# Projections of a hybrid trunk in four blocks of 448 columns and one of 288, in place of five of 416

## The chip, the cores and the metric

The kernel runs on one core of a Trainium2 chip. The metric is the device time of one launch in microseconds. A time is the median of several runs; beside it stands one profiled execution, whose trace is the source of all durations here.

## The reference

One layer of an encoder trunk, on T = 2080 rows of width 1024 (2048 prompt rows, 32 sample rows with their own history), all in fp32:

```python
hn = rmsnorm(h, g_mix)
proj = hn @ w_in                                   # 1024 x 3072
hA, bA, cA, zA, vB, zB = split(proj)               # six parts of 512
u = cA * hA                                        # conv mixer
yA = bA * (causal width-3 conv of u + bias) * silu(zA)
pooled = trailing mean of vB over 2/4/8/16 rows, by group of 128 channels, minus vB
yB = (pooled @ pool_w per group) * pool_scale * silu(zB)
h = h + concat[yA, yB] @ w_out
h = h + (p @ w_ple) * sigmoid(rmsnorm(h, g_ple) @ w_gate)
y = rmsnorm(h, g_final)
```

It also returns the last rows of u and v as states.

## The kernel before

**Numbers in two parts.** Every operand of a large matmul is split into a high and a low part (`split`, L77 to L79: ACT casts the high part, line 78; VectorE subtracts, line 79). A product of a 128-row slice is three matmuls (high by high, high by low, low by high). TensorE is named PE in the profile, with its weight loads as PEld.

**First stage, the projections.** The rows of x lie as columns in SBUF (normalised, transposed by `turn`, L416), in five blocks of `NB` = 416 columns. A block has three chunks of 128 rows and a short one of 32 (`x_rows`); the short chunks of two blocks share one tile (`columns_in`). A unit is one index j of four, that is 128 channels of each of the six parts zb, v, c, h, za, b. Blocks are taken in groups, `GROUPS = [[0, 1], [2, 3], [4]]`.

- Unit 0 of group 0 is computed as it stands (`plain`): 24 matmuls for each part and block (`project`, L581 and L564), 288 in all. Between its products the generator `second` prepares block 1, and `vectors` transposes the small vectors and splits the pool weights, all four groups of them at once (`pw`).
- The other seven units of groups 0 and 1 take both blocks of the pair at once by Strassen-Winograd (`seven`, `pair`): for each of the pairs (zb, v), (c, h), (za, b) seven half-products of 12 matmuls, 252 in a unit. Their right sides are six B pieces in three slots of the pool `acts`, and a seventh, T4, in `w7`. Names x_zbv, y_zbv, z_zbv and so on in the profile are these half-products' PSUM tiles.
- Group 2 is the last block alone, 384 prompt rows and the 32 sample rows, again by `plain`: 144 matmuls in a unit, in the order zb, v, c, h, the pool mixer's matmuls `pm` (method `mix`, L724 to L726), za, the states' transpose `pst`, b. Its columns were prepared by `last_block` beside group 1, chunk by chunk, and stored to memory (`b_d`); `hn_4` is read back at the start of group 2 by two loads on the POOL queue (L1140).

Within `plain` the pool mixer runs so: ACT copies v from PSUM to `V`; VectorE forms windowed sums (`win`, L746), `pl` (L758), and `pl` is split into `pp` (high and low part side by side in one tile); then `mix` multiplies by `pw` (three matmuls) and VectorE scales the result into `zs` (L728). The conv mixer multiplies h by c into `U` (L831), convolves (L771, L773), and multiplies by za and b (L844, L855). `store` writes `c_s` and `zs` to `y_d`.

VectorE and ACT also split each weight 10 us or so ahead of its use (`weights`, `put`; a ring of seven tiles), and in group 2 they form the sums of the output weights (`early_sums`, `weight_sums` L178) and the embedding weights `wp`.

**Later stages.** The output projection reads `y_d` back and does the same seven products with 512-wide matmuls (L168), then the embedding product (L103) and the gate follow. The change doesn't touch them, except that the first loads for the output stage (`load_y`, `load_rows`, `load_top`, pool `ya`) stand on the SP queue at the start of group 2.

The order of the instructions on each engine is set by a scheduler from the program; `keep_in_program_order` pins some of them. Every pool tile waits for the last readers of what lay there before; frames such as `frames_in` are closed to give their space to others.

## Time and profile before

| | |
|---|---|
| median of 3 runs | 922.03 us (920.8 to 922.24) |
| profiled execution | 923.96 us |
| its span, first to last instruction | 922.2 us |
| mean granted TensorE clock | 0.998 |
| 16.5 to 68.9 us | unit 0 |
| 68.9 to 426.4 us | the other seven units of groups 0 and 1 |
| 426.4 to 538 us | group 2, four units of about 27.9 us |
| 538 to 922 us | output projection, embedding, gate |

In a row of the windows stand, for each engine, the busy time and the number of instructions. In a row of the chain or the timeline stand the start, the length (from the first start to the last end of a run of like instructions) and their number; in brackets the idle time of the engine before them and what ended it. In the groups by line stand the busy time, the mean duration of one in ns, and the idle time before. A matmul's duration is longer than the distance between two starts, since matmuls are pipelined.

### The profile page before, as it was taken

Reading aid. Unit: us, or ns where it says so; the run is one execution under the profiler, and the core shown is the slowest. Engines: PE = TensorE matmul, PEld = TensorE weight load, DVE = VectorE, ACT = ScalarE, POOL = GpSimd, SP = SyncE. Lnnn points to the kernel's source line nnn. Section 1 sums busy time; section 2 is a strip of 40 time slices with the busy share of each in tenths; the row PEclk is TensorE's granted clock in tenths of the full one; section 3 lists DMA queues with packets and bytes.
Section 4 is the critical chain, followed back from the end, with each engine's and each line's share of the span. In section 5 each row is a group of like instructions: output and inputs, shape, how many; then the busy total and the mean of one; then the engine's idle time right before and its main releaser. Section 6 shows DMA issues by size and latency. Waiting matters only on the chain.

```text
span 922.2 us, 12940 instructions
## 1 busy us (share of the span) xinstructions
PE 907.6 (98%) x4485; PEld 820.7 (89%) x4485; DVE 723.1 (78%) x1231; ACT 477.8 (52%) x883; POOL 149.9 (16%) x271
## 2 busy tenths in 40 slices
PE   7999999999999999999999999999999999999996
PEld 5999999999999999999999987888877868888885
DVE  6896999999488989785777679665554799888975
ACT  6744565555335555443545456334334776465555
POOL 3111322212001111000000010111111002233333
PEclk9999999999999999999999999999999999999999
DMA  8345585769945546457655359755675876799883
GB/s 245 94 150 155 151 264 165 210 197 306 421 119 167 185 156 190 109 178 272 202 172 172 124 192 292 255 194 175 246 229 159 299 259 156 182 235 239 200 259 108
DMA packets 140734, 186.37 MB, mean 202 GB/s; under 512 B 12060, under 2 KB 111260, under 8 KB 139389
## 3 DMA queue, kind: packets, MB, share of 16 engines
q1 hardware_dynamic: 120237, 126.33, 44.7%
q0 software_dynamic: 17696, 53.71, 19.9%
q10 hardware_dynamic: 2736, 5.51, 1.8%
q8 instruction: 35, 0.57, 0.3%
q14 instruction: 30, 0.25, 0.1%
HBM read 128.93 MB, written 56.56 MB: 201 GB/s over the span
## 4 chain that ended last, share of the span: by engine, by line
PE 96%; ACT 1%; DVE 1%; DMA 1%; issue 0%; POOL 0%; SPq 0%; ACTq 0%; DVEq 0%; POOLq 0%
PE x_g L168 9%; PE x_o L168 9%; PE x_zbv L564 7%; PE x_ch L564 7%; PE x_zab L564 7%; PE e L103 5%; PE z_g L168 5%; PE z_o L168 4%; PE z_zbv L564 3%; PE z_ch L564 3%; PE z_zab L564 3%; PE v L564 3%; PE c L564 3%; PE b L564 3%; PE za L564 3%; PE h L564 3%
## 5 line engine op out<-in xcount | busy, mean ns | idle before, releaser
L78 ACT CAST y_S<-y_fS 128x512 fp32r<-128x512 f32 x32 | 19.5, 621 | 41.3 <-PE x_o L168 17.4
L103 PE MATMUL e<-wq,pps 128*128 128x512 f32 (+1 forms) x156 | 38.9, 399 | 0.2 <-ACT pps L78 0.2
L168 PE MATMUL x_o<-wo_b,y_S 128*128 128x512 f32 x128 | 35.7, 391 | 0.0
L168 PE MATMUL x_g<-wg_b,g_S 128*128 128x512 f32 x128 | 35.7, 389 | 0.0
L564 PE MATMUL z_zbv<-B,w_zbv_S 128*128 128x416 f32 x168 | 34.2, 352 | 0.0
L564 PE MATMUL x_ch<-B,w_ch_S 128*128 128x416 f32 x168 | 34.1, 351 | 0.0
L564 PE MATMUL z_zab<-B,w_zab_S 128*128 128x416 f32 x168 | 34.1, 351 | 0.0
L564 PE MATMUL x_zab<-B,w_zab_S 128*128 128x416 f32 x168 | 34.0, 351 | 0.0
L564 PE MATMUL x_zbv<-B,w_zbv_S 128*128 128x416 f32 x168 | 34.0, 351 | 0.0
L564 PE MATMUL z_ch<-B,w_ch_S 128*128 128x416 f32 x168 | 34.0, 350 | 0.0
L103 PEld LDWEIGHTS e<-wq,pps 128*128 128x128 f32 (+1 forms) x156 | 27.4, 182 | 6.9 <-ACT pps L78 0.5
L1396 POOL DMA_DIRECT2D e<-h_d x28 | 24.8, 907 | 51.1 <-DVE e L1393 42.3
L564 PEld LDWEIGHTS x_zab<-B,w_zab_S 128*128 128x128 f32 x168 | 31.3, 188 | 0.4
L564 PEld LDWEIGHTS x_zbv<-B,w_zbv_S 128*128 128x128 f32 x168 | 31.4, 188 | 0.3
L564 PEld LDWEIGHTS z_ch<-B,w_ch_S 128*128 128x128 f32 x168 | 31.4, 188 | 0.3
L564 PEld LDWEIGHTS z_zab<-B,w_zab_S 128*128 128x128 f32 x168 | 31.3, 188 | 0.3
L564 PEld LDWEIGHTS x_ch<-B,w_ch_S 128*128 128x128 f32 x168 | 31.3, 188 | 0.3
L564 PEld LDWEIGHTS z_zbv<-B,w_zbv_S 128*128 128x128 f32 x168 | 31.3, 188 | 0.4
L70 POOL TENSOR_SCALAR ms_x<-ssq_x 128x1 f32<-128x1 f32 (+2 forms) x18 | 10.7, 593 | 125.1 <-ACT junk L89 125.0
L78 ACT CAST y<-y 128x512 fp32r<-128x512 f32 x24 | 14.9, 619 | 29.3 <-PE z_o L168 12.8
L78 ACT CAST g_S<-g_fS 128x512 fp32r<-128x512 f32 x32 | 19.0, 618 | 18.6 <-DVE g_fS L1572 12.8
L168 PEld LDWEIGHTS x_o<-wo_b,y_S 128*128 128x128 f32 x128 | 24.0, 188 | 5.1 <-ACT c_o L1199 0.3
(592 smaller groups left out, 2656.6 us busy)
## 6 DMA issues: line engine op xcount, KB each, us to landing
y<-y_d SPq DMA_DIRECT2D x16, 512.0 KB, 5.6
x<-in_x_prompt_dram SPq DMA_DIRECT2D x16, 512.0 KB, 5.3
h_d<-x SPq DMA_DIRECT2D x16, 512.0 KB, 2.6
hn<-h_d SPq DMA_DIRECT2D x61, 128.0 KB, 6.5
xt<-in_x_prompt_dram SPq DMA_DIRECT2D x15, 512.0 KB, 6.1
e<-e_d SPq DMA_DIRECT2D x15, 512.0 KB, 6.0
e<-h_d POOLq DMA_DIRECT2D x28, 256.0 KB, 6.4
out_dram<-e POOLq DMA_DIRECT2D x13, 512.0 KB, 4.0
```

Source lines behind the costliest of these rows:

```text
L70: nc.gpsimd.tensor_scalar(ms[:n], ssq[:n], scalar1=1.0 / D, scalar2=EPS, op0=ALU.mult, op1=ALU.add)
L78: ins = nc.scalar.copy(hi, src)
L103: nc.tensor.matmul(ps[:n], pps[:, a, k, :n], wp[k][b][:, cs], start=k + q == 0, stop=k == 1 and q == 2)
L168: nc.tensor.matmul(ps[:n], lhs[:, k, a, :n], w[b][:, k], start=start and k + q == 0, stop=k == KH - 1 and q == 2, skip_group_check=True)
L564: nc.tensor.matmul(ps[:, :NB], lhs[:, k, x], b[:, k, y], start=start and k + q == 0, stop=stop and k == KH - 1 and q == 2, skip_group_chec ...
L1396: nc.gpsimd.dma_start(ee, h_d[r:r + P, at[1] * NH:at[1] * NH + NH], accum_op=ALU.add)
```

## The change

- `NB` is 448. The short chunk has `SH` = 64 rows; the last block has `NL` = 288 columns, two chunks of 128 prompt rows and the 32 sample rows, and `last_block` loops over three chunks, not four.
- The pool `acts` is closed with `frames_in` at the start of group 2 and opened again as `acts2` with smaller slots. T4 of the output weights has its eighth strip there (class `Strips`). The pools `acts2` and `ya` are opened with `reuse_waits="tile"`.
- The pool weight is loaded and split once for each unit (`load_pool_weight`, `pool_weight`). The low part of the pooled operand lies in a tile of the ring `e` (in group 2 behind the high part).
- In unit 0 `mix(0)` stands ahead of `v_block(1)`.
- `gm_row` lies in the ring `raws`; the staged short chunks take four tiles.

```diff
 EPS = 1e-6
-NB = 416
+NB = 448
+SH = NB - 3 * P
+NL = T - 4 * NB
 GROUPS = [[0, 1], [2, 3], [4]]
...
     w7 = ctx.enter_context(tc.tile_pool(name="w7", bufs=1))
-    SLOT = KC * 2 * NB
-    PIECE = SLOT // 2
+    PIECE = KH * 2 * NB
     def slot(name):
-        return acts[0].tile([P, SLOT], F32R, tag="hn", name=name)
+        return acts[-1].tile([P, 3 * KH * NH if len(acts) > 1 else 2 * PIECE], F32R, tag="hn", name=name)
+    class Strips:
+        def __init__(self, strips):
+            self.strips = strips
+        def __getitem__(self, at):
+            assert at[0] == slice(None)
+            return self.strips[at[1]]
...
     def seventh(name):
-        return w7.tile([P, 2 * KH * NH], F32R, tag="h", name=name)
+        return w7.tile([P, PIECE], F32R, tag="h", name=name)
...
         a, b = halves(slot(f"{name}_a")), halves(slot(f"{name}_b"))
-        t4 = seventh(f"{name}_T4").rearrange("p (h k n) -> p h k n", h=2, k=KH)
-        return dict(T1=a[:2], T2=(a[2], b[0]), T3=b[1:], T4=(t4[:, 0], t4[:, 1]))
+        t4 = seventh(f"{name}_T4")
+        t4 = [t4[:, i * NH:(i + 1) * NH] for i in range(2 * KH - 1)]
+        t4.append(acts[-1].tile([P, NH], F32R, tag="strip", bufs=1, name=f"{name}_T4_strip"))
+        return dict(T1=a[:2], T2=(a[2], b[0]), T3=b[1:], T4=(Strips(t4[:KH]), Strips(t4[KH:])))
...
         raws = pool("raws", 4)
-        acts.append(ctx.enter_context(tc.tile_pool(name="acts", bufs=3, side="right")))
         frames_in = ExitStack()
+        acts.append(frames_in.enter_context(tc.tile_pool(name="acts", bufs=3, side="right")))
         xin = frames_in.enter_context(tc.tile_pool(name="xin", bufs=5, side="right"))
...
-        gm_row = wk.tile([P, 2, 2 * NB], F32, tag="pp", bufs=1, name="gm_row").rearrange("p h n -> p (h n)")[:1, :D]
+        gm_row = ring4(raws, "gm_row")[:1]
         nc.sync.dma_start(gm_row, g_mix)
...
             r = tb * NB + c * P
-            if c < 3:
-                return x_p[r:r + P]
-            return x_p[r:r + DEC] if tb < 4 else x_s
+            if tb == 4:
+                return x_p[r:r + P] if c < 2 else x_s
+            return x_p[r:r + (P if c < 3 else SH)]
...
                     t = turn(xs[0], half, f"pt_{tag}_{half}", later=True)
-                    yield [t[:, :, :DEC], t[:, :, DEC:2 * DEC]]
+                    yield [t[:, :, :SH], t[:, :, SH:2 * SH]]
...
                 yield
-            n = P if len(xs) == 2 else DEC
+            n = P if len(xs) == 2 else SH
             f12, f1, f21 = (ftile(f"{c}_{tag}")[:, :, :n] for c in ("f12", "f1", "f21"))
...
         p_d = {q: tc.dram_tile([P, KH, 2, NB], F32, name=f"p_d{q}") for q in NAMES}
-        b_d = tc.dram_tile([P, KC, 2, NB], F32, name="b_d")
+        b_d = tc.dram_tile([P, KC, 2, NL], F32, name="b_d")
...
                 for q, (x, y) in enumerate(((0, 0), (0, 1), (1, 0))):
-                    nc.tensor.matmul(ps[:, :NB], lhs[:, k, x], b[:, k, y], start=start and k + q == 0,
+                    nc.tensor.matmul(ps[:, :b.shape[-1]], lhs[:, k, x], b[:, k, y], start=start and k + q == 0,
                                      stop=stop and k == KH - 1 and q == 2, skip_group_check=True)
...
             normal(x)
-            n = P if c < 3 else DEC
+            n = P if c < 3 else SH
             for half, q in enumerate(("11", "21")):
...
                 normal(x, True)
-            xs.append((short0, slice(DEC, 2 * DEC)))
+            xs.append((short0, slice(SH, 2 * SH)))
             yield
...
         vec = const.tile([P, 112], F32, name="vec")
-        pw = one.tile([P, 2, 4, P], F32R, name="pw")
+        pw_raws = []
+        def load_pool_weight(j):
+            t = one.tile([P, P], F32, tag="pw_raw", name=f"pw_raw_{j}")
+            nc.sync.dma_start(t, pool_w[0, j])
+            pw_raws.append(t)
+        def pool_weight(j):
+            t = one.tile([P, 2, P], F32R, tag="pw", name=f"pw_{j}")
+            split(t[:, 0], t[:, 1], pw_raws.pop())
+            load_pool_weight((j + 1) % 4)
+            return t
         rows = ftile("rows").rearrange("p k n -> p (k n)")[:112, :P]
...
             nc.vector.tensor_copy(vec, pv[:, :112])
-            split(pw[:, 0], pw[:, 1], pw_raw)
...
-        pw_raw = raws.tile([P, 4, P], F32, tag="t", name="raw_pw")
-        nc.sync.dma_start(pw_raw, pool_w[0].rearrange("g c d -> c g d"))
+        load_pool_weight(0)
-        def etile(name, n=NB):
-            return wk.tile([P, 2 * NB + 16], F32, tag="e", bufs=2, name=name)[:, :n]
+        def etile(name, n=NB, dtype=F32):
+            return wk.tile([P, 2 * NB + 16], dtype, tag="e", bufs=2, name=name)[:, :n]
...
                 self.L = min(SEQ - tbs[0] * NB, len(tbs) * NB)
+                self.n = NB if len(tbs) > 1 else NL
                 self.last = tbs[-1] == 4
...
-                lo, hi = bs[0] * NB, bs[-1] * NB + NB
+                lo, hi = bs[0] * self.n, (bs[-1] + 1) * self.n
                 if self.last and bs[-1] == len(self.tbs) - 1:
...
             def cols(self, t, b):
-                return t[:, b * NB:(b + 1) * NB]
+                return t[:, b * self.n:(b + 1) * self.n]
...
                 r = self.tbs[b] * NB
-                nc.sync.dma_start(y_d[chunk, :, r:r + NB], self.cols(t, b))
+                nc.sync.dma_start(y_d[chunk, :, r:r + self.n], self.cols(t, b))
...
-                pp, j = self.cols(self.pooled.rearrange("p h n -> p (h n)"), b), self.j
-                pq = self.pooled[:, 1, b * NB:b * NB + NB]
+                j, n, pw = self.j, self.n, self.pw
+                pp = self.cols(self.pooled, b)
+                pq = self.rest[b]
                 pm = tbank(f"pm_{self.tag}_{b}")
-                nc.tensor.matmul(pm[:, :NB], pw[:, 0, j], pp, start=True, stop=False)
-                nc.tensor.matmul(pm[:, :NB], pw[:, 0, j], pq, start=False, stop=False)
-                nc.tensor.matmul(pm[:, :NB], pw[:, 1, j], pp, start=False, stop=True)
+                nc.tensor.matmul(pm[:, :n], pw[:, 0], pp, start=True, stop=False)
+                nc.tensor.matmul(pm[:, :n], pw[:, 0], pq, start=False, stop=False)
+                nc.tensor.matmul(pm[:, :n], pw[:, 1], pp, start=False, stop=True)
                 z = self.cols(self.zs, b)
-                nc.vector.scalar_tensor_tensor(z, pm[:, :NB], pscale(j), z, op0=ALU.mult, op1=ALU.mult)
+                nc.vector.scalar_tensor_tensor(z, pm[:, :n], pscale(j), z, op0=ALU.mult, op1=ALU.mult)
                 self.store(4 + j, b, self.zs)
...
                 if self.pooled is None:
-                    self.pooled = wk.tile([P, 2, 2 * NB], F32R, tag="pp", bufs=1, name=f"pp_{self.tag}")
+                    self.pw = pool_weight(j)
+                    self.pooled = wk.tile([P, 2 * NB], F32R, tag="pp", bufs=1, name=f"pp_{self.tag}")
+                    self.rest = {}
                 for seg in self.segs(*bs):
...
                                                    op0=ALU.mult, op1=ALU.subtract)
-                    parts = self.pooled[:, 0, lo:hi], self.pooled[:, 1, lo:hi], pl
+                    if self.last:
+                        self.rest[0] = self.pooled[:, self.n:2 * self.n]
+                        lows = self.rest[0][:, lo:hi]
+                    else:
+                        lows = etile(f"pq_{self.tag}_{tb}", m, F32R)
+                        for i, b in enumerate(bs):
+                            self.rest[b] = lows[:, i * self.n:(i + 1) * self.n]
+                    parts = self.pooled[:, lo:hi], lows, pl
                     if late is None:
...
                     project(ps, w, tbs[b], between)
-                    return ps[:, :NB]
+                    return ps[:, :self.n]
...
                 def v_block(b):
-                    ps, o = product_of("v", b, wv), b * NB
+                    ps, o = product_of("v", b, wv), b * self.n
                     for seg in self.segs(b):
...
                         zb_block(b)
-                        v_block(b)
                         if b:
                             self.mix(b - 1)
+                        v_block(b)
+                        if b:
                             next(second)
...
                         lo, hi = seg[:2]
-                        o = b * NB
+                        o = b * self.n
                         nc.vector.tensor_tensor(self.place(U, 2, seg), ps[:, lo - o:hi - o], c_s[:, lo:hi], op=ALU.mult)
...
-                places = iter(t[:, :, :, i * DEC:(i + 1) * DEC] for t in map(staged, ("short_0", "short_1")) for i in range(4))
-                dst = lambda q, src, n: to_memory(p_d[q], f"{q}_1_{c}", src, c * P, n, next(places) if n == DEC else None, True)
+                places = iter(t[:, :, :, i * SH:(i + 1) * SH] for t in map(staged, ("short_0", "short_1", "short_2", "short_3")) for i in range(2))
+                dst = lambda q, src, n: to_memory(p_d[q], f"{q}_1_{c}", src, c * P, n, next(places) if n == SH else None, True)
                 for i, _ in enumerate(frame_sums(ahead.pop((1, c)), f"g1_{c}", dst)):
...
                 x = x_stat(ahead.pop((2, c))[0], True)
-                if c < 3:
+                if c < 2:
                     load_ahead(2, c + 1)
...
-            for c in range(5):
-                n = scale(c) if c < 4 else 0
+            for c in range(4):
+                n = scale(c) if c < 3 else 0
                 yield
...
-        xs_d = tc.dram_tile([NB, D], F32, name="xs_d")
+        xs_d = tc.dram_tile([NL, D], F32, name="xs_d")
...
                 frames_in.close()
-                t = slot("hn_4")
-                hn[4] = piece_of(t, 0), piece_of(t, 1)
+                acts.append(ctx.enter_context(tc.tile_pool(name="acts2", bufs=3, side="right", reuse_waits="tile")))
+                t = slot("hn_4")[:, :KC * 2 * NL].rearrange("p (k h n) -> p k h n", k=KC, h=2)
+                hn[4] = t[:, :KH], t[:, KH:]
                 for half in range(2):
...
                 nc.sync.dma_start(g_bc, g_fin.partition_broadcast(P))
-                ya = ctx.enter_context(tc.tile_pool(name="ya", bufs=5, side="right"))
+                ya = ctx.enter_context(tc.tile_pool(name="ya", bufs=5, side="right", reuse_waits="tile"))
                 first_y = load_y(0, 2 * P)
```

More of the change, by code (lines that the diff above doesn't have):

```diff
@@ L803, in plain @@
                         zb_block(b)
+                        if b:
+                            self.mix(b - 1)
                         v_block(b)
                         if b:
-                            self.mix(b - 1)
                             next(second)
```

## The prediction

> **What bounds the kernel now.** I read the page's busy shares and chain first, then the windows by stage, then single rows where a term of the sum is made.
>
> ```profile
> span 922.2 us, 12940 instructions
> PE 907.6 (98%) x4485; PEld 820.7 (89%) x4485; DVE 723.1 (78%) x1231; ACT 477.8 (52%) x883; POOL 149.9 (16%) x271
> PE 96%; ACT 1%; DVE 1%; DMA 1%; issue 0%; POOL 0%; SPq 0%; ACTq 0%; DVEq 0%; POOLq 0%
> ```
>
> TensorE is busy 98% and holds 96% of the chain, so what counts is the number of matmuls times the spacing of their starts, plus whatever makes PE wait. By stage (unit 0; the units of groups 0 and 1; the four units of group 2 one by one; the output projection):
>
> ```profile
> core 0: us, PE busy (x) PEld busy (x) DVE busy (x) ACT busy (x) POOL busy (x), PEclk, DMA share, GB/s
> 16.50:68.90 52.40, 52.40 (x280) 51.34 (x281) 49.01 (x93) 31.79 (x64) 8.23 (x10) 1.00 0.45 133
> 122.00:426.40 304.40, 304.10 (x1623) 300.12 (x1622) 260.52 (x436) 151.62 (x274) 41.50 (x57) 1.00 0.66 211
> 426.40:454.30 27.90, 27.90 (x150) 27.54 (x149) 19.21 (x48) 12.83 (x26) 2.03 (x4) 1.00 0.72 203
> 482.00:510.00 28.00, 28.00 (x151) 27.63 (x150) 20.50 (x47) 13.12 (x26) 1.99 (x4) 1.00 0.55 166
> 510.00:538.00 28.00, 28.00 (x152) 27.57 (x151) 20.00 (x43) 12.14 (x24) 2.00 (x4) 1.00 0.31 105
> 538.00:710.00 172.00, 171.25 (x749) 136.78 (x747) 111.27 (x173) 74.94 (x131) 24.06 (x49) 1.00 0.71 225
> ```
>
> The second number of a row is PE's busy time. From 16.5 us to 538 PE has practically no gap (0.3 us in 304), at full clock. That is the whole stage the change rewrites. The cover differs: VectorE has 6 to 10 us to spare in each unit of group 2, which the change will use up.
>
> **The matmuls.** Their number stays: 2052 in groups 0 and 1 (288 in the plain unit 0, then 7 units of 252), 576 in group 2 (4 units of 144), and 60 of `pm`. Only widths change: 416 to 448 in groups 0 and 1, 416 to 288 in group 2. The spacing, from the chain's rows and a timeline of 256-wide matmuls near the end:
>
> ```profile
> 77.95 2.27 PE x_zbv L564 x12
> 426.45 4.53 PE zb L564 x24
> 771.75 2.72 PE z_g L168 x12
> 912.92 1.59 PE L103 MATMUL e_l<-wl,pps_l 128*128 128x256 f32 x12
> 912.70 1.61 PEld L103 LDWEIGHTS e_l<-wl,pps_l 128*128 128x128 f32 x12
> L103 PE MATMUL e_l<-wl,pps_l 128*128 128x256 f32 x12 | 1.6, 282 | 0.0
> L564 PEld LDWEIGHTS z_ch<-B,w_ch_S 128*128 128x128 f32 x168 | 31.4, 188 | 0.3
> ```
>
> 416 wide: 4.53/24 = 188.9 ns. 512 wide (`z_g`): 2.72/12 = 226.7. 256 wide (`e_l`): the twelve span 1.59 us, the last one lasting about 0.282, so (1.59-0.282)/11 = 119 to 120 ns. A straight line through 256 and 512 is columns/2.4 + 13.3; the 416 row lies 2.2 ns above it. Both rows on the line are multiples of 64 columns, 416 and 288 are not, 448 is. So I take 448 on the line, 200.0 ns, and 288 above it, 133.3 + 2.2 = 135.6. Then
> - groups 0 and 1: 2052 x (200.0 - 188.9) = +22.8 us;
> - group 2: 576 x (135.6 - 188.9) = -30.7 us;
> - `pm`: 48 x 11.1 - 12 x 53.3 = -0.1 us.
>
> Together **-8.0 us**. Bounds: with 288 on the line too, -9.3; with 448 at the 416 row's excess (202.2), -3.5. That last value is what the columns alone give: 2052 x 32 more and 576 x 128 fewer, some 8,000 columns at 1/2.4 ns. What lies above it is a bet on the 2.2 ns.
>
> The Trainium skill (TensorE: Matmul & The Clock Gate, Back-to-back issue gap) gives the warm spacing as N/2.4 + 2.5 ns, one constant for all widths; by it the gain is the columns' alone, near -3.4. The trace has 188.9 for 416 columns where that rule gives 175.8, so its constant does not hold here, but a constant of any size gives the same gain. That is a rival below.
>
> **The start.** The short piece of a block has 64 columns where it had 32, two of them share one tile, and so its transposes become full ones:
>
> ```profile
> 12.97 1.97 PE L416 MATMUL pt<-ident,xt 128*128 128x128 f32 x8 [0.66 <-DVE xt L407]
> 15.40 1.08 PE L416 MATMUL pt<-ident,xt 64*128 64x64 f32 x8 [0.46 <-PE pt L416]
> ```
>
> Eight transposes before the first matmul take 1.97 us instead of 1.08: +0.9, all of it on the path, since nothing else is ready for PE. Their copies to SBUF move twice the elements, and some more transposes later are wider: I add 0.4. **+1.3 us** (0.9 to 1.7).
>
> **Unit 0.** `mix(0)` goes ahead of `v_block(1)`; its operand was ready long before. `mix(1)` stays behind `c(1)`, and the later `v` end stands at the same distance. Its chain on VectorE:
>
> ```profile
> 45.79 0.58 DVE L746 TENSOR_TENSOR win<-V 128x416 f32<-128x416 f32 x1
> 46.29 0.64 DVE L728 SCALAR_TENSOR_TENSOR zs<-pm,vec,zs 128x416 f32<-128x416 f32 x1
> 48.56 0.58 DVE L79 TENSOR_TENSOR pp<-pl,pp 128x416 fp32r<-128x416 f32 x1
> 50.18 0.19 PE pm L724
> ```
>
> `pp` was ready at 49.1, 1.1 us before `pm` at 50.2. Without the three `pm` between, PE arrives 0.6 us sooner, and each pass is 5% longer: **+0.3** (0 to 0.7). The per-unit split of the pool weight (one cast, one subtraction of 128x128) lies on ACT and VectorE, which have room in groups 0 and 1 (260.5 of 304.4 us busy); its cost there is nothing, and 12 extra pairs at a few tenths of a us each if that room were gone. The same holds for the larger elementwise passes of these units, which grow by 8% at most while PE grows by 6%.
>
> **Loads of the second group and of the last block.** A B piece grows from 1664 to 1792 KB (+8%):
>
> ```profile
> B<-p_d POOLq DMA_DIRECT2D x3, 1664.0 KB, 12.0
> hn<-b_d POOLq DMA_DIRECT2D x2, 1664.0 KB, 8.8
> 415.42 1.11 POOL L1140 DMA_DIRECT2D hn<-b_d  x2 [29.60 <-PE y_zab L564]
> 417.22 2.43 PE L564 MATMUL z_zab<-B,w_zab_S 128*128 128x416 f32 x12
> DMA to landing us min/median/max: 7.0/8.8/10.7
> 426.29 4.70 PE L564 MATMUL zb<-hn,w_zb 128*128 128x416 f32 x24
> ```
>
> The B loads have PE's unbroken run as evidence of slack; 8% of 12 us is 1 us each, cost nothing (1 us if there is no slack). The last block's load `hn` is another matter. It waited for the second of the seven products (`y_zab`, ended by 415.4); landings 7.0 and 10.7 us after issue, against first use at 426.3 and 2.3 us later. With the buffers laid out anew its slot overlaps two pieces of B that the fourth product (`z_zab`, starting 417.22) still reads, so it is issued two products later, with three products (3 x 2.40 = 7.2 us) to go, and the second half is wanted 12 x 0.136 = 1.6 us after. It moves 288/416 of the bytes: 7.0 and 10.7 become about 5 and 7.5. Against 7.2 and 8.8 that is hidden, but the loads of the output stage on the SP queue now start in the same window. **+0.3**, between 0 and 2.6 (the second landing not shortened, and 0.7 lost at its issue: 10.7 + 0.7 - 8.8).
>
> **Group 2: where the gain meets VectorE.** A unit's PE time falls from 27.9 to 144 x 0.1356 + 3 x 0.1356 + 0.1 = 20.0 us. VectorE had 19.2 to 20.5. Some ten of its passes a unit are as wide as the block, and narrow by 128 columns at about 1 ns each (684 ns at 512 against 590 at 416): -1.3, and the pool weight's subtraction adds 0.3. So 18 to 19.5 us: 95% of PE. VectorE's spare time in these units is gone with it. What is late next is `pm`, which PE must issue in program order behind `h`:
>
> ```profile
> 440.05 4.53 PE h L564 x24
> 443.39 0.19 DVE L79 TENSOR_TENSOR pp<-pl,pp 128x32 fp32r<-128x32 f32 x1
> 444.58 0.19 PE pm L724
> 519.12 4.53 PE c L564 x24
> 519.67 0.58 DVE L746 TENSOR_TENSOR win<-V 128x398 f32<-128x398 f32 x1 [1.39 <-ACT V L792]
> 525.95 0.19 DVE L79 TENSOR_TENSOR pp<-pl,pp 128x32 fp32r<-128x32 f32 x1
> 527.19 0.69 DVE L178 TENSOR_TENSOR wo_r<-wo_r 128x512 f32<-128x512 f32 x1
> 528.19 0.19 PE pm L724
> ```
>
> From the end of `v` (start of `c`) to `pm` PE works 9.06 us on `c` and `h`; the pooled operand `pp` is whole 8.1 us after the end of `v` in the first unit (435.52 to 443.58) and 7.0 in the last (519.12 to 526.14). After the change the window is 48 x 0.1356 = 6.5 us. In the changed program's order, VectorE's list from the first `win` to the last `pp` holds 10, 14, 18 and 20 instructions in the four units, among them the weight halves of the next unit and the sums of the output weights. At the durations above, less 0.08 us of overlap each, that is 4.7, 6.6, 8.4 and 8.4 us, behind 0.6 us for the copy of `V`. In units 2 and 3 even `U`, which needs `h`, stands ahead of the last `pp`. Against 6.5: 0, 0.4, 1.2 and 2.4 us of PE waiting (in the longer lists part is saved because the queue starts ahead of time). **+4.0 us**, from 1.5 (only the `U` order costs, 0.7 each twice) to 9 (lists fully exposed, 0.7 + 2.5 + 2.5, and 3 for ACT's casts in between). Behind the waiting `pm`, PE's whole queue stands: `za`, `b` and the next unit.
>
> **After group 2.** VectorE ends its list up to 4 us behind PE, with the output stage's weights and the last `c_s` in it. That stage has gaps of its own on PE (172.00 - 171.25 = 0.75) and VectorE is idle 3.06 us at its start:
>
> ```profile
> 538.42 0.59 DVE L855 TENSOR_TENSOR c_s<-b,c_s 128x416 f32<-128x416 f32 x1
> 547.07 0.69 DVE L148 COPY eout<-e 128x512 f32<-128x512 f32 x1 [3.06 <-PE e L103]
> ```
>
> That idle time takes most of it: **+0.5** (0 to 2).
>
> **Sum:** -8.0 + 1.3 + 0.3 + 0.3 + 4.0 + 0.5 = **-1.6 us**. The profiled execution took 923.96 us (its span and 1.8 around it), 1.9 above the median of 922.03. Taken off the median: **920.4 us**.
>
> **The rivals.**
> - **The spacing's extra is one constant.** 448-wide matmuls then start every 202.2 ns. For it: the 416 row, 32 columns away, has that excess; against: 512 wide, 64 away, does not. The price is 2052 x 2.2 = 4.5 us: **925**, slower than before. It decides from a spacing of 200.8 on, where the widths no longer outweigh the rest of the sum (+6.4); from 201.7 on the loss can be measured.
> - **VectorE takes the bound of group 2**, its list whole ahead of every `pm`: stalls of 9 us instead of 4, **925.4**. For it: 18 to 19.5 us busy of 20, and an order fixed for a 28 us unit; against: today it is idle 7 us a unit waiting for ACT and transfers, which can shrink.
> - **No stall at all**: `pp` comes in time, since VectorE works ahead. -8.0 + 2.4 = **916.4**. Against: `U` ahead of `pp` in two units.
> - **Weight loads bound narrow matmuls.** Every load's record is 188 ns, near the 416 spacing. Then 288 also costs 188, group 2 gains nothing and stalls nowhere: 22.8 + 0.5 + 2.4 = +25.7, **947.7**. Against: `e_l`, twelve loads of 190 ns in 1.61 us at 256 columns.
> - **The last block's load is late**: 2.6 us instead of 0.3, **922.7**, no change.
>
> **How the numbers follow.** Forecast with the terms as chosen 0.40, its own range 918 to 923; one constant 0.20; VectorE bound 0.20; no stall 0.13; weight loads 0.02; late load 0.05. About 0.2% (1.8 us) is what a measurement of this kernel can tell from no change. The forecast's 0.40 lies at that border: 0.22 faster, 0.15 the same, 0.03 slower. With no stall 0.13 faster and a little of the rivals (0.05): faster 0.40; same 0.15 and 0.05 of the late load, 0.20; slower 0.40. The range holds no stall with 288 on the line (915) and both 925s with a further 2 us for the output stage: 914.5 to 928.
>
> **What would show it.** Spacing of `x_zbv` at 448 columns: 12 in 2.40 us (2.43 by the rival). `zb` of the last block: 24 in 3.25 us (4.5 if loads bound). Ahead of `pm` in group 2: PE idle near 0, 0.4, 1.2, 2.4, released by `pp`. First `zb` of the last block without a wait. The first matmul 1.3 us later than 16.49. I am wrong if the spacing at 448 is over 201, if group 2's four units take more than 87 us in all, or if PE's idle time appears outside the start and `pm`.

## The result and the profile after

The changed kernel takes 931.36 us (median of 6 runs, 928.9 to 933.65), the kernel before on the same chip 922.13 (6 runs, 920.8 to 923.7): a ratio of 1.0099, 95% interval 1.0082 to 1.0115. It is 9.2 us slower. The profiled execution took 930.78 us with a span of 929.0, 6.8 above the span of before.

Busy shares and the chain of the page after:

```profile
PE 906.7 (98%) x4485; PEld 791.6 (85%) x4485; DVE 726.0 (78%) x1235; ACT 480.0 (52%) x890; POOL 148.2 (16%) x266
PE 86%; DMA 6%; DVE 5%; ACT 2%; issue 1%; DVEq 0%; ACTq 0%; SPq 0%
```

TensorE's busy time is 1 us less for the same number of matmuls, and TensorE's part of the chain falls from 96% to 86%: transfers and VectorE have entered it. Windows of the kernel after, in order: unit 0 and the Strassen units, the four units of group 2, the output projection. Columns as before (the second number is PE's busy time, the number after the POOL column its clock):

```profile
core 0: us, PE busy (x) PEld busy (x) DVE busy (x) ACT busy (x) POOL busy (x), PEclk, DMA share, GB/s
16.50:454.60 438.10, 438.10 (x2188) 403.07 (x2188) 362.86 (x607) 215.93 (x397) 58.39 (x76) 1.00 0.56 174
454.60:482.20 27.60, 22.16 (x150) 21.71 (x150) 16.69 (x45) 12.58 (x27) 2.04 (x4) 0.88 0.77 256
482.20:502.60 20.40, 20.08 (x150) 19.59 (x149) 17.04 (x45) 12.01 (x27) 1.62 (x4) 1.00 0.70 211
502.60:523.70 21.10, 19.89 (x150) 19.63 (x149) 18.20 (x49) 11.90 (x27) 2.38 (x5) 1.00 0.73 218
523.70:545.20 21.50, 20.46 (x155) 20.17 (x154) 17.95 (x46) 10.96 (x24) 0.92 (x2) 1.00 0.66 208
545.20:765.50 220.30, 219.05 (x974) 171.94 (x973) 150.18 (x242) 114.42 (x213) 25.86 (x54) 1.00 0.73 235
```

The account by stage, from the starts of the first matmul of each stage in both traces:

| stage | before | after | difference |
|---|---|---|---|
| up to the first matmul of unit 0 | 16.42 | 16.02 | -0.4 |
| unit 0 and the Strassen units | 409.87 | 438.61 | +28.7 |
| group 2, to the embedding's first matmul | 112.1 | 90.6 | -21.5 |
| everything behind it | 383.8 | 383.8 | 0.0 |

So there are two places. The Strassen stage has no gap at all (438.10 us busy of 438.10), yet it costs 5 us more than the widths were taken to cost. Group 2 gives 21.5 us where its widths alone give 31, and one unit of the four loses nearly all of the rest: 27.6 us, no shorter than before, at a clock of 0.88.

**The spacing.** Rows of the chain in the Strassen stage, each twelve matmuls of 448 columns:

```profile
399.34 2.48 PE x_zab L577 x12
401.82 2.48 PE x_zbv L577 x12
434.06 2.48 PE x_ch L577 x12
437.77 2.43 PE x_zab L577 x12
```

Not 2.40 us but two values: 2.43 (202.7 ns between starts) and 2.48 (206.7). The sum over the trace of all distances from a projection's matmul to the next start grows from 392.0 to 419.8 us in this stage, 204.6 ns on average, breaks included. Without the breaks the mean distance is 203.9 ns, against 188.9 at 416 columns, which alone makes +30.8 us. The breaks were shorter after the change, in part by luck: the trace of before has TensorE still at half clock when unit 0 begins, and its first eight matmuls take 3.14 us, against 2.05 in the trace of after.

**The first unit of group 2.** PE's timeline at the wait, then VectorE's, then the SP queue's:

```profile
456.22 1.75 PE L577 MATMUL v<-hn,w_v 128*128 128x288 f32 x12
461.37 2.94 PE L577 MATMUL c<-hn,w_c 128*128 128x288 f32 x21
472.93 0.61 PE L749 MATMUL pm<-pp,pw 128*128 128x288 f32 x1 [5.44 <-ACT pp L80]
474.02 5.04 PE L577 MATMUL za<-hn,w_za 128*128 128x288 f32 x24
```

```profile
460.94 0.69 DVE L81 TENSOR_TENSOR w_za<-raw_za,w_za 128x512 fp32r<-128x512 f32 x1 [1.54 <-ACT w_za L80]
468.89 0.69 DVE L180 TENSOR_TENSOR wo_r<-wo_r 128x512 f32<-128x512 f32 x1 [7.26 <-DMA wo_r<-in_w_out_dram]
469.50 0.42 DVE L773 TENSOR_TENSOR win<-V 128x256 f32<-128x256 f32 x1
473.14 0.18 DVE L81 TENSOR_TENSOR pp<-pl,pp 128x32 fp32r<-128x32 f32 x1
```

```profile
449.86 4.04 SPq L328 DMA_DIRECT2D y<-y_d  x2
457.41 2.55 SPq L333 DMA_DIRECT2D wo_q<-in_w_out_dram  x4
461.16 2.28 SPq L1036 DMA_DIRECT2D wo_r<-in_w_out_dram  x2
```

The narrow matmuls are as fast as hoped: twelve in 1.75 us with the last one lasting 0.294, so (1.75 - 0.294)/11 = 132.4 ns. But `pm` waits 5.44 us for `pp`, until 472.93. VectorE had lost its time before: from 461.6 to 468.9 it stood 7.26 us in front of `wo_r`, a tile of the output weights that was still in flight, and only then came to `win`, `pl` and `pp`, which stand behind it in its list.

`wo_r` was late because it was issued late. The SP queue of the kernel before shows the same loads here:

```profile
388.25 0.92 SPq L315 DMA_DIRECT2D y<-y_d  x2
389.76 2.04 SPq L320 DMA_DIRECT2D wo_q<-in_w_out_dram  x4
425.59 0.34 SPq L1000 DMA_DIRECT2D wo_r<-in_w_out_dram  x1
```

There the output stage's first loads (`y`, `x`, `wo_q`) had gone out 38 us ahead of group 2 (426.29), not at its start, and `wo_r` just ahead of it. In the changed kernel the buffers are laid out anew: `y` now waited for `z_zab`, the last product that reads B pieces, and went out from 449.86 on, and `wo_r` stood behind these loads until 461.16, 6.5 us after the start of group 2 (454.63). VectorE could go on 14.3 us after that start, where it had been 5.3. Behind the wait of `pm` TensorE ran at half clock for a while: `za` took 5.04 us where `zb` and `v` take about 3.3. The rule of the Trainium skill (TensorE: Matmul & The Clock Gate, HAM oscillation) that TensorE's idle gaps over about 3.4 us bring the clock down agrees with the 0.88 of this window; the waits of 0.3 to 1.2 us in the next three units left it at 1.00. But shorter waits than that can do it too: in the run with the late loads, below, a single wait of 1.9 us in the second unit came with a clock of 0.93.

### The profile page after: what moved, and what is told of

Its sections match the earlier page's. It is cut to its first block, busy times and chain, and to the rows that moved or that the text cites. A ratio compares the mean times of both kernels' runs of the same rounds, so it can differ in the third digit from the quotient of the medians.

```text
span 929.0 us, 12953 instructions
## 1 busy us (share of the span) xinstructions
PE 906.7 (98%) x4485; PEld 791.6 (85%) x4485; DVE 726.0 (78%) x1235; ACT 480.0 (52%) x890; POOL 148.2 (16%) x266
## 4 chain that ended last, share of the span: by engine, by line
PE 86%; DMA 6%; DVE 5%; ACT 2%; issue 1%; DVEq 0%; ACTq 0%; SPq 0%
PE x_o L170 9%; PE x_g L170 9%; PE x_zbv L577 7%; PE x_ch L577 7%; PE x_zab L577 7%; PE z_g L170 5%; PE z_o L170 4%; PE z_ch L577 4%; PE z_zbv L577 4%; PE z_zab L577 4%; PE e L105 3%; PE y_g L170 2%; PE y_o L170 2%; PE za L577 2%; DMA wo_r<-in_w_out_dram 2%; PE y_ch L577 2%
## 5 line engine op out<-in xcount | busy, mean ns | idle before, releaser
L80 ACT CAST y_S<-y_fS 128x512 fp32r<-128x512 f32 x32 | 19.5, 621 | 40.7 <-PE x_o L170 16.9
L577 PE MATMUL z_zbv<-B,w_zbv_S 128*128 128x448 f32 x168 | 36.7, 367 | 0.0
L577 PE MATMUL z_zab<-B,w_zab_S 128*128 128x448 f32 x168 | 36.7, 367 | 0.0
L577 PE MATMUL x_ch<-B,w_ch_S 128*128 128x448 f32 x168 | 36.6, 367 | 0.0
L577 PE MATMUL z_ch<-B,w_ch_S 128*128 128x448 f32 x168 | 36.6, 366 | 0.0
L577 PE MATMUL x_zab<-B,w_zab_S 128*128 128x448 f32 x168 | 36.5, 366 | 0.0
L577 PE MATMUL x_zbv<-B,w_zbv_S 128*128 128x448 f32 x168 | 36.5, 366 | 0.0
L72 POOL TENSOR_SCALAR ms_x<-ssq_x 128x1 f32<-128x1 f32 (+1 forms) x17 | 12.5, 738 | 117.3 <-ACT junk L91 117.0
L80 ACT CAST y<-y 128x512 fp32r<-128x512 f32 x24 | 14.8, 619 | 29.6 <-PE x_o L170 14.1
```

The source lines that it names most:

```text
L72: nc.gpsimd.tensor_scalar(ms[:n], ssq[:n], scalar1=1.0 / D, scalar2=EPS, op0=ALU.mult, op1=ALU.add)
L80: ins = nc.scalar.copy(hi, src)
L577: nc.tensor.matmul(ps[:, :b.shape[-1]], lhs[:, k, x], b[:, k, y], start=start and k + q == 0, stop=stop and k == KH - 1 and q == 2, skip_g ...
```

## The experiments

Ratios are against the kernel before, from runs on the same chip in the same session. Line numbers are those of each run's own kernel. In the expectations, theory A is that loads queued ahead of `wo_r` make it late, and theory B that VectorE's list of work is too long for the narrow unit.

### Widths, and the cause of the spacing

```diff
+        width = [NB]
...
+                    m = b.shape[-1] if k + q == 0 else min(b.shape[-1], width[0])
-                    nc.tensor.matmul(ps[:, :b.shape[-1]], lhs[:, k, x], b[:, k, y], start=start and k + q == 0,
+                    nc.tensor.matmul(ps[:, :m], lhs[:, k, x], b[:, k, y, :m], start=start and k + q == 0,
...
                 unit = gi * 4 + j
+                width[0] = (448, 416, 432, 440, 400, 384, 352, 320, 288, 272, 256, 280)[unit]
```

> Leaves out columns: within each half-product all matmuls but the first one take only the first m columns, with m set per unit: 448 in unit 0, then 416, 432, 440 in the other units of group 0, 400, 384, 352, 320 in group 1, and 288, 272, 256, 280 in group 2. What is read is the distance between starts in each unit, not the time. One constant for all widths (the excess of the 416 row, 15.6 ns): 432 at 195.6, 440 at 198.9, 400 at 182.3, 384 at 175.6, 352 at 162.3, 320 at 148.9. Line through 256 and 512 columns (13.3 ns): 384 at 173.3, 352 at 160.0, 320 at 146.7, 400 at 180.0, with an extra only where a matmul lasts about as long as a weight load's record (188 ns), so at 416 to 448. Weight loads as a floor: nothing under 188. If the slow spacing of 206.7 ns belongs to 448 columns alone, no unit but the first shows a second value.

Mean distance between the starts of neighbouring matmuls of one width, from the starts in the trace (288 from the changed kernel, 256 and 512 from the kernel before; the narrow units of this run were full of waits and are not used):

| columns | 256 | 288 | 320 | 352 | 384 | 400 | 416 | 432 | 440 | 448 | 512 |
|---|---|---|---|---|---|---|---|---|---|---|---|
| ns | 119.3 | 132.4 | 146.4 | 160.3 | 174.1 | 180.6 | 188.5 | 195.8 | 200.2 | 202.7 or 206.7 | 226.7 |
| over columns/2.4 | 12.6 | 12.4 | 13.1 | 13.6 | 14.1 | 13.9 | 15.2 | 15.8 | 16.9 | 16.0 or 20.0 | 13.3 |

Neither a constant nor the question of 64 columns orders these numbers. (The slope between 256 and 512 columns is 2.4 columns per ns, so columns/2.4 is the columns' own time.) The extra is nearly flat up to 400 columns, 12 to 14 ns, rises from 416 to 448 and is back at 13 at 512. The widths that suffer are those that stream for about as long as a weight load's record lasts (188 ns is 451 columns at that slope); that the two disturb each other is the reading that fits, but only the place of the hump is shown, not the mechanism. Weight loads as a floor are refuted: 132.4 ns at 288.

### What sets the second value

```diff
                 i = 0
+                tc.keep_in_program_order(nc.tensor.transpose(tbank(f"dummy_{self.tag}")[:, :P], ident, ident))
                 while i < 3:
```

> The changed kernel with one transpose of the identity, read by nobody, ahead of each of the seven Strassen units (0.1 us each). What is read is where the 448-wide matmuls start every 202.7 ns and where every 206.7. If the spacing is a pattern that is chosen anew at each interruption of the run of equal matmuls and then held, the long stretch at 206.7 from 384 to 437 us is cut at the start of its last unit (near 405 us) or moves, and no unit changes in the middle of an uninterrupted run. If it depends on the data, the buffers or the transfers of that time, the stretches stay where they were to within 1 us.

The chain of this run at the start of the last Strassen unit:

```profile
401.44 2.48 PE x_zab L577 x12
403.92 0.11 PE dummy L990
404.02 2.43 PE x_zbv L577 x12
```

In the changed kernel the same place (401.82) went on at 2.48, up to the next `pm` at 436.5. One transpose that computes nothing ends it; the next 2.48 begins behind a `pm` at 439.3, where the changed kernel has 2.43. So which of the two spacings holds is set when something breaks the stream, and it is kept until the next break. A break can be a few other matmuls, a single transpose, or a short wait: at 346 us of the changed kernel the spacing turned from 206.7 to 202.7 behind two longer distances (0.27 and 0.31 us), with no other matmul between. What follows a break is not fixed by the program. The run with `wo_r` in `ya` (below) has the same matmuls in the same order up to group 2; it ran at 206.7 from 349 to 384 us and at 202.7 from 385 to 436, where the changed kernel has 202.7 and then 206.7. The single time, 930.05 us, is no more than the changed kernel's.

### The loads of the output stage moved away

```diff
-                first_y = load_y(0, 2 * P)
-                first_x = load_rows(ya, "x", 0, x_p)
-                tops = [ring4(ya, f"wo_q{i}") for i in range(2)]
-                for k in range(KH):
-                    load_top(k, tops[k // 2])
...
                 if gi == 2:
                     early_sums(j)
+                if unit == 9:
+                    first_y = load_y(0, 2 * P)
...
```

(the six lines together, their loads kept in program order)

> The first loads of the output stage (y_0, x, four wo_q) are issued after the second unit of group 2 and not at its start. Theory A, the queue: the wait of 5.4 us ahead of the first pm and the half clock after it come from wo_r, which stood behind these loads on the SP queue and held VectorE's list. Then the first unit's wait falls under 1 us, the clock stays at 1.00 there, and the time is 931.4 - 5.4 - 1.7 = 924.3 us (923 to 926). Theory B, VectorE's list is simply too long for the narrow unit: the first unit still waits 2 us or more, and the time stays at 928 or above. A third outcome: the loads, now ahead of the third unit's weights, hold those up, and a wait of some 3 us appears there.

Ratio 1.0079 (1.0050 to 1.0108), median 930.8 us: hardly better. Windows of its first two units:

```profile
457.50:481.90 24.40, 21.63 (x149) 21.16 (x148) 17.71 (x47) 12.13 (x27) 2.04 (x4) 0.93 0.64 196
481.90:505.20 23.30, 21.39 (x150) 21.07 (x149) 16.70 (x47) 11.11 (x25) 1.74 (x4) 0.93 0.99 299
```

The first unit took 24.4 us in place of 27.5, but the second one, into which the loads have moved (DMA share 0.99), 23.3. In the first, VectorE could now go on with `wo_r` 5.2 and 11.6 us after the start of group 2, and still stood in front of it, 3.44 and 2.43 us. Theory A holds for part of the wait only.

### The pool mixer's matmuls one product later

```diff
                 if len(tbs) == 1:
-                    self.mix(0)
                     st = self.states()
...
                     nc.vector.tensor_tensor(c, c, z, op=ALU.mult)
...
+                if len(tbs) == 1:
+                    self.mix(0)
                 wb = weights("b", j, f"b{tag}")
```

> In group 2 the pool mixer's matmuls stand behind the product za (3.2 us of TensorE) and not behind h; nothing else is changed. Theory A: the three short waits (0.3, 1.2, 1.0 us) go, and of the long one 3.2 us are covered, with its half clock shortened: 931.4 - 2.5 - 3.2 - 0.5 = 925.2 us (924 to 928). Theory B, VectorE is the bound of these units: the wait only moves to za's or b's operands or to the next unit, and the time stays within 2 us of 931.4.

Ratio 1.0105 (1.0082 to 1.0127). The first unit took 29.0 us: 2.06 us ahead of `pm`, and 3.77 ahead of the states' transpose, which waits for `U` in the same list. The wait had only moved, as theory B said; but VectorE again stood before `wo_r` in that unit, for 7.05 us, so this doesn't speak for B's cause.

> Both edits together: late loads, and pm behind za. Theory A: no wait over 0.5 us is left in group 2, its four units take 4 x 20.0 = 80 us and some, and the time is 931.4 - 7.1 - 2.5 = 921.8 us (920.5 to 924), about that of the kernel before: what is then left of the expected gain went to the spacing of the 448-wide matmuls. Theory B: group 2 stays above 86 us and the time above 926.

Both edits: ratio 1.0069 (1.0046 to 1.0092), median 929.9. Group 2 took 87.8 us, 2.8 less than in the changed kernel, but 2.1 of that came back behind it (385.9 us against 383.8). VectorE in the first unit:

```profile
460.22 0.69 DVE L180 TENSOR_TENSOR wo_r<-wo_r 128x512 f32<-128x512 f32 x1 [2.92 <-DMA wo_r<-in_w_out_dram]
466.40 0.69 DVE L180 TENSOR_TENSOR wo_r<-wo_r,wo_r 128x512 f32<-128x512 f32 x1 [2.25 <-DMA wo_r<-in_w_out_dram]
```

That is 4.7 and 10.9 us after the start of group 2 (455.55). The kernel before has the same two waits:

```profile
431.57 0.69 DVE L178 TENSOR_TENSOR wo_r<-wo_r 128x512 f32<-128x512 f32 x1 [3.48 <-DMA wo_r<-in_w_out_dram]
436.28 0.69 DVE L178 TENSOR_TENSOR wo_r<-wo_r,wo_r 128x512 f32<-128x512 f32 x1 [1.71 <-DMA wo_r<-in_w_out_dram]
```

5.3 and 10.0 us after its start of group 2 (426.29). With the output stage's loads out of the way the transfer is as late as it was in the kernel before. What is left of the change is when its work is wanted: `pm` came 18.3 us after the start of group 2 (444.58); in the narrow unit it is due after 4 x 3.2 = 12.8, and behind `za` after 16.0.

### More room for wo_r

```diff
-            raw = [ring4(raws, f"wo_r{k}_{i}") for i in range(2)]
+            raw = [ring4(ya, f"wo_r{k}_{i}") for i in range(2)]
...
-                if unit == 9:
+                if unit == 11:
```

(on top of both edits; the second line puts the output stage's loads behind the last unit)

> As the run with both edits, and the rows of the output weights (wo_r) now go through the five tiles of the pool ya, which the late loads leave empty until the last unit; the four tiles of the ring raws then carry the units' own weights alone. Theory C, the feed: a unit of group 2 needs eight 512 KB tiles through a ring of four, each some 5 us in flight and held until VectorE has split it, and that is what the 20 us unit runs into; with wo_r out of the ring the waits go, group 2 takes 80.5 to 82 us from its first matmul to the embedding's and the time is 929.9 - 6 = 924 us (922 to 925.5). Theory B, VectorE's list as such: group 2 stays at 86 us or more, the time at 928 or more. If the output stage's loads come too late, that shows as PE idle time after group 2, not within it.

Ratio 1.0075 (1.0051 to 1.0099). Windows of its first two units:

```profile
454.70:482.10 27.40, 22.21 (x150) 21.34 (x149) 22.99 (x58) 14.53 (x31) 2.03 (x4) 0.88 0.98 323
482.10:501.70 19.60, 19.60 (x150) 19.57 (x150) 19.55 (x50) 13.55 (x29) 1.58 (x4) 1.00 0.87 251
```

(The profiled run is the fastest of the five, 926.7 us against a median of 930.5.) With a ring of their own the loads of `wo_r` went out early for several units at once, and VectorE made the passes of two units ahead of the first `win`: 22.99 us of work in the first unit. The last three units lost nothing (19.6, 19.5, 20.3 us), although VectorE is busy for 19.55 of 19.60 us in the second. So VectorE's list is not too long for a unit of this width: theory B falls for the steady state. The first unit lost as much as ever, and theory C (the ring of four) explains the small waits of the later units only.

### 432 columns

```diff
-NB = 448
+NB = 432
...
-        return w7.tile([P, PIECE], F32R, tag="h", name=name)
+        return w7.tile([P, max(PIECE, 7 * NH)], F32R, tag="h", name=name)
...
-                return x_p[r:r + P] if c < 2 else x_s
+                return x_p[r:r + P] if c < 2 else x_p[r:SEQ]
...
-[x_load(f"4_{c}", [x_rows(4, c)])]
+[x_load(f"4_{c}", [x_rows(4, c)] + [x_s] * (c == 2))]
```

> The changed kernel with one size altered: four blocks of 432 columns and one of 352. From the spacings measured in the run of widths (432: 195.8 ns, 352: 160.3; 416: 188.9, 448: 203.9, 288: 133.2) the projections' matmuls take 2052 x 195.8 + 576 x 160.3 = 494.1 us, against 496.4 with 416 alone and 495.1 with 448 and 288. A unit of group 2 is 23.6 us of TensorE. If the loss of the changed kernel in group 2 comes from units shorter than their feed (theories B and C alike), most of its 10 us go here: waits of 0 to 4 us in all, time 920 to 925 us. If it came from the new buffers whatever the width, the waits stay near 8 us and the time at 928 or above.

Ratio 1.0137 (1.0112 to 1.0162), a miss. The first two units of its group 2:

```profile
439.50:472.00 32.50, 25.87 (x150) 25.06 (x149) 18.70 (x49) 12.56 (x27) 2.04 (x4) 0.89 0.84 271
472.00:495.60 23.60, 23.60 (x150) 23.53 (x149) 18.98 (x46) 12.79 (x27) 1.99 (x4) 1.00 0.73 206
```

The wider unit does not help the first one: here `wo_r` let VectorE go on at 455.1, 15.6 us after the start of group 2, just when `pm` was due (4 x 3.86 = 15.4). The 432-wide matmuls started every 196.5 ns, and the output stage took 5 us longer than in the changed kernel (225.6 against 220.3 us), which was not looked into.

> 432 and 352 columns with the late loads, pm behind za and wo_r in the pool ya. No wait over 0.5 us in group 2: 922.1 - 2.3 + 0.5 for the wider short pieces = 920.3 us (918.5 to 922). By theory B it stays above 923.

Ratio 1.0154 (1.0136 to 1.0172), with 36.4 us in the first unit. A miss too.

### The sums of the output weights one unit later

```diff
-                nc.sync.dma_start(raw[i], w_out[(i * KH + k) * P:(i * KH + k + 1) * P])
+                tc.keep_in_program_order(nc.sync.dma_start(raw[i], w_out[(i * KH + k) * P:(i * KH + k + 1) * P]))
```

(on top of the run with wo_r in ya)

> As the run with wo_r in the pool ya, and the loads of wo_r are kept in program order, behind the unit's own loads: the sums of the output weights of unit j now stand in VectorE's list of unit j + 1, the last ones after group 2, and the first y_0, x and wo_q follow them. So the first unit of group 2 has none of this work in it. Theory D, the first unit: in every variant so far the first unit lost 6 to 8 us and the three others under 1.5 each, because at the start of group 2 VectorE stops at a wo_r that is still in flight, with win, pl and pp behind it in its list. Then the first unit takes 20.1 to 21 us in place of 27, group 2 80.5 to 83, with the clock at 1.00 throughout, and the time is 6 us under the run with wo_r in ya (930.5): 924.5 us (922 to 926.5), 1 to 2 more if the output stage now waits for its first loads. Theory B, VectorE's list as such: the wait only moves to the units that now carry the sums; group 2 stays at 86 us or more.

Ratio 1.0223 (1.0203 to 1.0242). Windows of the first two units, and PE at the start of the output stage:

```profile
454.60:474.10 19.50, 19.50 (x149) 19.47 (x148) 14.09 (x41) 10.41 (x23) 2.03 (x4) 1.00 0.81 235
474.10:497.30 23.20, 21.63 (x150) 21.12 (x149) 17.73 (x45) 12.27 (x27) 2.01 (x4) 0.93 0.62 181
```

```profile
564.57 1.65 PE L165 MATMUL x_o<-wo_c,y 128*128 128x512 f32 x3 [16.59 <-ACT y L80]
```

Theory D's first half is as expected: without `wo_r` in its list the first unit takes 19.5 us at full clock. The rest is not: the second unit now meets the transfer, and the output stage starts 16.6 us late, because its own loads have come last in the queue.

```diff
-            raw = [ring4(ya, f"wo_r{k}_{i}") for i in range(2)]
+            raw = [ring4(ya if k < 3 else raws, f"wo_r{k}_{i}") for i in range(2)]
...
-                if unit == 11:
+                if unit == 10:
```

> As the run before (sums of the output weights one unit late), with the output stage's first loads (y_0, x, wo_q) now issued at the end of the third unit of group 2, behind the last unit's weights, and the last set of wo_r in the ring raws. By theory D both halves of the loss are avoided: the first unit of group 2 without a wait as in that run, and the output stage starting as in the changed kernel, 8.5 to 9 us after the embedding's first matmul in place of 25. Group 2 takes 82 to 84.5 us, the rest 383.8, the part before it 454.6: a span of 921.5 to 923.5 and a time of 923 to 926 us, some 6 to 8 us under the changed kernel, and level with the kernel before or 1 to 2 us above it, since the spacing of the 448-wide matmuls (204.6 ns with all breaks) has taken what the narrow block gives. If the output stage's loads hold up the last unit's weights, a wait of 2 to 4 us shows in the last unit and the time is 927 or more.

Ratio 1.0126 (1.0107 to 1.0145). The same 19.6 and 23.4 us in the first two units, and still 3.75 us of waiting ahead of the output projection, with 1.6 ahead of the embedding. Each order of the same transfers loses somewhere else.

### The transfer itself taken away

```diff
-            raw = [ring4(raws, f"wo_r{k}_{i}") for i in range(2)]
+            raw = [ring4(raws if k else ya, f"wo_r{k}_{i}") for i in range(2)]
             for i in range(2):
+                if not k:
+                    nc.gpsimd.memset(raw[i], 0.5)
+                    continue
```

(on top of both edits)

> The run with both edits (late loads, pm behind za), in which the first two tiles of wo_r are filled by a memset on POOL and not loaded: 1 MB less through the SP queue and the ring in the first unit of group 2; a quarter of the output weights' rows is thereby left out. VectorE's passes over them stay, ahead of win in its list. If the first unit is lost to the transfer (VectorE standing before a tile in flight), it now takes 20 to 21.5 us in place of 25.5, with the clock at 1.00, and the time falls by 4 to 6 us from 929.9: 924 to 926. If it is lost to VectorE's passes as such, the first unit stays at 24 us or more and the time within 2 us of 929.9.

Ratio 0.9996 (0.9980 to 1.0012), median 922.0 us of 10 runs. Group 2 of this run:

```profile
455.10:474.70 19.60, 19.60 (x150) 19.57 (x149) 18.04 (x49) 12.27 (x27) 2.04 (x4) 1.00 0.81 236
474.70:494.20 19.50, 19.50 (x149) 19.46 (x149) 16.52 (x43) 11.47 (x25) 1.47 (x3) 1.00 0.96 297
494.20:514.50 20.30, 19.91 (x150) 19.59 (x149) 15.97 (x41) 12.18 (x27) 1.64 (x5) 1.00 0.71 211
514.50:536.40 21.90, 20.98 (x157) 20.30 (x155) 19.50 (x51) 11.28 (x24) 1.94 (x4) 1.00 0.70 212
```

VectorE makes the same passes over `wo_r` ahead of `win` (18.04 us busy in the first unit, against 18.16 with the load), and the first unit runs without a gap. The gain is the first unit's: it took 25.6 us with the load, while the others took 19.6, 20.7 and 21.9, about as here. This settles the loss that both edits had left in group 2: it is the transfer (with the place that it takes in the queue and in the ring, which the run doesn't tell apart), not VectorE's passes. It also shows what the widths give once nothing waits. Group 2 in some 81 us instead of 112 is -31, the Strassen stage +28.7 in the changed kernel: 2 to 3 us by the traces (span 920.1 against 922.2, though the profiled run of before lay 1.9 us above its median), nothing that the medians can tell from the kernel before.

## Why the prediction was wrong, point by point

- **The spacing of 448 columns** (taken on the line at 200.0 ns, "multiples of 64") was wrong. The stage's matmuls cost +27.8 us, not +22.8. The point at which this prediction said it would be wrong (201 ns) was passed. The first rival came near the lower of the two spacings (202.2, +27.3 us), but not for its reason: the extra is no constant over the widths, and part of the stage ran at 206.7. That the stage's sum is so near the rival's +27.3 is luck: the spacing alone is worth +30.8, and shorter breaks gave 3 back.
- **288 columns** at 135.6 was too slow: 132.4, some 2 us better than the term of -30.7.
- **Group 2's waits** were the larger error: +4.0 was forecast, and 9.8 us are missing (21.5 gained against the 31.3 of the terms for the matmuls and `pm`), some 8 us idle ahead of the four `pm` and the rest in matmuls at half clock. The limit of 87 us for group 2 was passed too (90.6). The step that failed is the start of VectorE's list: it was taken to begin 0.6 us behind `v`, and its durations were summed as if each pass could start when the one before ended. In the first unit the list itself was not longer than forecast (3.8 us from the first `win` to the last `pp`, against 4.7), but it began 8.1 us behind `v` (469.50, where PE goes on to `c` at 461.37). In place of VectorE's work the runs show a wait for a transfer ahead of it, 7.26 us for `wo_r`. The wait had two causes. The output stage's loads, which the new buffers hold back, stood ahead of `wo_r` on the queue; taking them away shortened the first unit from 27.5 to 24.4 us. The rest was in the trace of before: VectorE waiting 3.48 and 1.71 us for `wo_r` in the same place, at no cost to TensorE. The prediction counted such waits as time that "can shrink"; the transfer took as long beside the shorter unit. The second rival had the size (9 us), with VectorE's work as its cause, which the run without the transfer refutes.
- **Which unit** was wrong too: the waits were forecast to grow from 0 in the first unit to 2.4 in the last; they were 5.44, 0.31, 1.21 and 1.04. That the output stage's loads start in that window was noted for `hn` alone, while `wo_r` stands behind them on the same queue.
- **The last block's load** was right: `zb` started without a wait. **The output stage** (+0.5) took 383.8 us as before. **Unit 0** cost no wait.
- **The start** (+1.3) came out at -0.4. The eight wide transposes took 1.06 us, as the narrow ones had:

```profile
8.49 5.57 PE L429 MATMUL pt<-ident,xt 128*128 128x128 f32 x24 [2.28 <-DVE xt L420]
14.93 1.06 PE L429 MATMUL pt<-ident,xt 128*128 128x128 f32 x8 [0.87 <-PE pt L429]
```

The row it was priced by, 1.97 us for eight, was of TensorE at a lower clock: the first rows of this run have 1.97 for eight as well.

- **The range** ended at 928 because the two rivals of 925 were treated as alternatives. They are independent: -1.6 + 4.5 + 5.0 = +7.9, near the measured 9.2.

What stays open: why the spacing has its hump near 448 columns and why two values exist there; and a version faster than both kernels was not found.

## What to carry to other kernels

Read the spacing of a new matmul width from a run of that width, or from rows on both sides of it, before a gain is summed over thousands of matmuls. When a stage is made shorter, look in the old trace for every wait on a transfer in it, on any engine's list: the work shrinks with the stage and the transfer does not, so a wait that cost nothing can come to stand ahead of the bound. Two rivals that act in different stages add, and the range has to hold their sum.

## What the runs showed of the hardware

- Of equal matmuls with a weight load each, those of 416 to 448 columns start 15 to 20 ns after the columns' own time, those of 256 to 400 and of 512 columns 12 to 14.
- 448-wide matmuls have two spacings, 202.7 and 206.7 ns. One of them holds over long stretches (206.7 from 384 to 436 us of the changed kernel) and changed only at a break: other matmuls, a single transpose, or a short wait (two distances of 0.27 and 0.31 us). With the same order of matmuls, two runs had opposite spacings in the same two stretches.
- The granted clock fell in units whose longest wait of TensorE was 1.9 us (0.93, loads moved away), 3.2 (0.87, both edits) and 5.4 (0.88, changed kernel); a unit with one wait of 1.2 us kept 1.00 (changed kernel), and one with two waits of 0.7 and 0.9 us had 0.93 (sums one unit later). The length of a single wait does not order these.
